# A conv input projection as block pairs of seven products, with modulation sums moved, residual parts added by DMA and fills removed

## The chip, the cores and the metric

The kernel runs on one core of a Trainium2 chip. The metric is the device time of one execution in microseconds. The core has five engines that run beside each other: TensorE (PE, matmuls into PSUM), VectorE (DVE), ScalarE (ACT), GpSimd (POOL) and SyncE (SP, which issues most loads). DMAs run on 16 DMA engines that all issuing queues share.

## The reference

A small diffusion transformer of two layers over 256 latent tokens and 256 context tokens, d = 1024, everything in float32. The kernel works on both streams side by side, as 512 columns (`T2`), the latent half first (`S` = 256 each). What matters here:

```python
def _modulate(t, g, shift, scale):
    return _rms(t, g) * (1 + scale) + shift

def _swiglu(h, w13, w2):
    gte, up = jnp.split(h @ w13, 2, axis=-1)
    return (jax.nn.silu(gte) * up) @ w2

def _short_conv_mixer(h, w_in, k, w_out):
    bgate, cgate, xv = jnp.split(h @ w_in, 3, axis=-1)
    return (bgate * _dwconv3(cgate * xv, k)) @ w_out

for i in range(DEPTH):   # layer 0: short conv; layer 1: attention
    mod  = (jax.nn.silu(c) @ mod_w[i] + mod_b[i])       # 9 chunks of d: shift, scale, gate x 3
    lat = lat + 0.5 * gate0 * _swiglu(_modulate(lat, ...), ffn_w13[i, 0], ffn_w2[i, 0])
    lat = lat + gate1 * mixer(_modulate(lat, ...))
    lat = lat + 0.5 * gate2 * _swiglu(_modulate(lat, ...), ffn_w13[i, 1], ffn_w2[i, 1])
    # the context stream cx goes the same way, up to the attention of layer 1
```

`_dwconv3` is a convolution of width 3 along the tokens, channel by channel.

## The kernel before

**Products.** Every float32 operand is split into a high part `hi` (rounded to the format that PE takes in one pass) and a low part `lo` = x - hi: ACT writes `hi` (L107), DVE writes `lo` (L108). One product is then three matmuls, hi hi, lo hi, hi lo (`mm3`, L136 to L138). Activations lie transposed, channels on partitions, so one matmul takes 128 channels by 512 columns (both streams) or 256 (one).

**Stages.** In order: a first stage written out by hand (`FIRST_STEPS`: modulation by PE, first norm, first three FFN blocks); FFN (0,0); the conv mixer; FFN (0,1); FFN (1,0); attention; FFN (1,1) on the latents alone. An FFN goes in thirds of 8, 7 and 7 hidden blocks: the blocks' gate and up products, then a `project` that multiplies them by that third of `w2`, eight output blocks m, and adds each to the residual `x` in `finish` (two `scalar_tensor_tensor` of 128x256 on DVE, L563, out of PSUM, times the modulation gate). In the last third `finish` also runs a `tail`: squares and sums for the next norm, which normalises one stream while PE still does the last two m of the other.

**Block pairs of seven products.** `Pair` computes a gate block and an up block together. Weights are seen as a 2x2 matrix of blocks (two halves of the 1024 input channels by two output blocks), activations as a 2x2 matrix (two halves of channels by two streams), and the product of these takes seven block products for eight, in the manner of Strassen and Winograd: A11, A12, S1 to S4 and A22 with B11, B21, T1 to T4 and B22. One product is 4 x 3 matmuls of 256 columns. The sums cost work elsewhere: per pair POOL negates a piece and issues two accumulating DMAs (L701, L704, L114), DVE makes the weight sums (L723, L731) and splits them (L108), and combines results in `six`, `seven` and `four` (L760, L765, L771); ACT copies partial results out of PSUM (L748, L754, L758). `Blocks.sums` makes T1 to T4 once per stage. A stage that uses pairs begins with two blocks multiplied plainly, stream by stream, while the norm of the second stream and the T sums come in; in between, the first pair's weights are made.

**The conv input before.** `h` is a `Plain` (hi and lo of each channel block). For each m of 8: three products of 8 channel blocks, `pv`, `pc`, `pb` (24 of `mm3`; for m = 0 stream by stream, otherwise 512 columns), then ACT copies `pv` (L1160), DVE multiplies (L1162), ACT and DVE apply the three taps (L1164, L1167, L1171), DVE multiplies by `pb` (L1176) and the result `z` is split. Then `project` with `conv_w_out`.

**Modulation sums.** 224 of them: DVE reduces a row block of `mod_w` (128x1024, 512 KB loaded per pair of sums) with the conditioning vector (L177). `tick(n)` spreads them: each call adds n to an account and issues a sum for each whole unit; `tick(ev)` stands in `project` for the first m. What is still missing when a gate or norm needs its chunk is issued there and then (`gate_of`, `scale_of`, through `mod_ready`).

**Fills.** `fill(n)` issues n matmuls on a tile of ones into an unused bank (L896): 12 at the start (`WARM`), 2 in each of four `add` of `first_sums`, and the steps F2, F2, F4, F5 of `FIRST_STEPS`.

**Order.** Apart from the first stage and the attention heads, a scheduler with a cost model orders each engine's instructions, and pools hand out buffers in that order: 8 for raw weights (`wr`), 4 each for `wh` and `wl`, 3 each of the 128x512 tags `sg` and `gm`, 6 PSUM banks.

Of the kernel before, what the change touches and what calls it, by code (L numbers as in the profile page):

```python
# [16 lines left out]
P = 128  # L17
D = 1024
# [18 lines left out]


FIRST_STEPS = (
# [9 lines left out]
def hybrid_kernel(ctx: ExitStack, tc: tile.TileContext, a: dict, out: bass.AP):  # L49
# [56 lines left out]
    def split(hi, lo, src):  # L106
        nc.scalar.activation(out=hi, in_=src, func=AF.Copy)  # L107
        return nc.vector.tensor_tensor(out=lo, in0=src, in1=hi.bitcast(F32), op=ALU.subtract)  # L108
# [261 lines left out]
    def pick(h, k, c0, c1):  # L370
        return h.at(k, c0, c1)
# [184 lines left out]

    def finish(m, ps, c0, c1, gate, tail, wide=False):
        g = gate(m)
        for s in range(2):
            for o in [s * S - c0] if not wide else range(0, T2 if s == 0 else 0, S):  # L560
                if not c0 <= s * S < c1:
                    continue
                ins = nc.vector.scalar_tensor_tensor(  # L563
                    out=x[:, m, s * S : s * S + S],
                    in0=ps[:, o : o + S],
                    scalar=g[:, m, s : s + 1],
                    in1=x[:, m, s * S : s * S + S],
                    op0=ALU.mult,
                    op1=ALU.add,
                )  # L570
        if tail:
            tail(m, c0, c1)
        return ins.ins

    def ready():

# [111 lines left out]
    class Pair:  # L688
# [67 lines left out]
        def six(self):  # L756
            self.prod(self.p, "S2", "T2", False)
            nc.scalar.copy(self.sg[:, S:], self.p)  # L758
            self.prod(self.q1, "S4", ("B", 1, 1), False)
            nc.vector.tensor_tensor(out=self.sg, in0=self.q, in1=self.sg, op=ALU.add)  # L760
            nc.scalar.activation(out=self.sg, in_=self.sg, func=AF.Silu)  # L761

        def seven(self):
# [4 lines left out]

        def four(self, g):
            self.prod(self.p, "A22", "T4", False)  # L770
            nc.vector.tensor_tensor(out=self.gm, in0=self.sg, in1=self.u, op=ALU.mult)  # L771
            split(g[0], g[1], self.gm)

    def ffn(l, b, h, tot, gate, tail, gs=(), ev=(0, 0), z=None):
        gs = list(gs)
        i0 = 0
        for t, n in enumerate(THIRDS):
            between = ()
            if tot == T2:
                heads = []  # L780
                if t == 0 and not gs:

                    w = [load_w(a["w13"][l, b, 0])]
                    gs = [new_pair("g") for _ in range(2)]
                    pp = [(psum("pg"), psum("pu")) for _ in range(2)]
                    w13_mm(pp[0], w[0], h, range(KT), 0, S)
                    flush(1)
                    w.append(load_w(a["w13"][l, b, 1]))
                    at = w13_mm(pp[1], w[1], h, range(2), 0, S)
                    with tc.issue_after(at):  # L790
                        flush()
                    with tc.issue_after(every[-1]):
                        w13_mm(pp[1], w[1], h, range(2, KT), 0, S)
                    h.sums(0)
                    w13_mm(pp[0], w[0], h, range(KT), S, T2)
                    w13_post(pp[0], gs[0], 0, T2)
                    heads.append(Pair(a["w13"][l, b, 2], h))
                    h.sums(1)
                    heads[0].sums(0)
                    w13_mm(pp[1], w[1], h, range(KT), S, T2)  # L800
                    w13_post(pp[1], gs[1], 0, T2)
                    heads[0].head()
                    heads[0].sums(1)
                    h.sums(2)
# [336 lines left out]
    zs = []  # L1141
    for m in range(KT):
        wcx = load_w(a["cw_cx"][m])
        if m % 2 == 0:
            wb = load_w(a["cw_b"][m // 2])
        pc, pv, pb = psum("pc"), psum("pv"), psum("pb")
        for c0, c1 in ((0, S), (S, T2)) if m == 0 else ((0, T2),):
            groups = ((pv, wcx, P), (pc, wcx, 0), (pb, wb, (m % 2) * P))
            if m == 0:
                order = [(k, *g) for k in range(KT) for g in groups[:2]]  # L1150
                for k in range(KT):
                    order.insert(min(10 + 3 * k, len(order)), (k, *groups[2]))
            else:
                order = [(k, *g) for g in groups for k in range(KT)]
            for n, (k, ps, w, off) in enumerate(order):
                mm3(ps[:, c0:c1], w(k * 256 + off), pick(h, k, c0, c1), k == 0, k == KT - 1)
                if n == 11:
                    flush()
        xv = tp.tile([P, T2], F32, name=nm("xv"), tag="sg", bufs=3)
        nc.scalar.copy(xv, pv)  # L1160
        u = tp.tile([P, T2], F32, name=nm("u"), tag="gm", bufs=3)
        nc.vector.tensor_tensor(out=u, in0=xv, in1=pc, op=ALU.mult)  # L1162
        d = tp.tile([P, T2], F32, name=nm("d"), tag="gm", bufs=3)
# [7 lines left out]
        nc.vector.scalar_tensor_tensor(  # L1171
            out=d2[:, :, : S - 1], in0=u2[:, :, 1:], scalar=convk[:, 2, m : m + 1],
            in1=d2[:, :, : S - 1], op0=ALU.mult, op1=ALU.add,
        )
        z = tp.tile([P, T2], F32, name=nm("z"), tag="sg", bufs=3)
        nc.vector.tensor_tensor(out=z, in0=d, in1=pb, op=ALU.mult)  # L1176
        zs.append(new_pair("z"))
        split(zs[m][0], zs[m][1], z)
        tick(5)

    def by_pairs(key, box=None):
        box = box or {}
# [6 lines left out]

        return ws  # L1190

    hn = Blocks()
# [282 lines left out]
def _layout(inp):  # L1475
# [30 lines left out]
        axis=2,  # L1506
    )
    ci = f("conv_w_in")[0]
    cx = ci[:, D:].reshape(KT, P, 2, KT, P)
    d["cw_cx"] = cx.transpose(3, 1, 0, 2, 4).reshape(KT, P, 2048)  # L1510
    d["cw_b"] = kp(ci[:, :D], 256)
    d["cw_out"] = kp(f("conv_w_out")[0], 256)
# [41 lines left out]
```

## Time and profile before

| | |
|---|---|
| three runs, median (lowest, highest) | 1552.14 us (1551.94, 1553.91) |
| profiled execution | 1552.53 us |
| its span on the core | 1550.8 us |
| busy: PE, DVE, ACT, POOL | 1542.2, 1281.7, 781.8, 223.0 us |
| matmuls | 10238 |
| conv input, first matmul to first matmul of the output projection | 378.5 to 511.3 us |

Busy time of PE overlaps from matmul to matmul, so its pace is read from the distance between starts and not from durations. A window gives, for a stretch in microseconds from the span's start, its length, each engine's busy time (with the count of instructions), the granted TensorE clock, and the mean busy share of the 16 DMA engines.

### The profile page before, as it was taken

The page shows a single profiled execution, that of the slowest core. Times are in us where ns is not written, and L with a number is a line of the kernel's source. Part 1 is how long each engine was busy: PE and PEld are TensorE (multiplying, and loading weights), DVE is VectorE, ACT ScalarE, POOL GpSimd, SP SyncE. Part 2 cuts the span into 40 slices and gives each one's busy share as a digit, 9 for nine tenths or more (in the row PEclk, how much of TensorE's full clock was granted, in tenths as well). Part 3 has the DMA queues.
Part 4 walks back from the last instruction along what each step waited for, and adds up shares of the span by engine and source line. Part 5 has one row for each costly group of instructions (what it writes and reads, how often), then busy time and mean ns, then how long its engine had stood idle before and what let it go on. Part 6 is the DMA issues. An engine that isn't in the chain of part 4 may idle for free.

```text
span 1550.8 us, 26218 instructions
## 1 busy us (share of the span) xinstructions
PE 1542.2 (99%) x10238; PEld 1414.8 (91%) x10238; DVE 1281.7 (83%) x1998; ACT 781.8 (50%) x1294; POOL 223.0 (14%) x187
## 2 busy tenths in 40 slices
PE   9999999999999999999999999999999999999999
PEld 7898998998888899989999899989999899998888
DVE  4888789799987589968978889968978878888676
ACT  5742553544423366436346476436346456774553
POOL 0012213200000112032042112022042002300000
PEclk9999999999999999999999999999999999999999
DMA  9567467475564425655656635655766753376562
GB/s 372 203 184 190 114 187 195 118 197 170 182 208 167 115 63 136 205 145 134 204 144 163 198 75 137 203 150 128 231 174 175 258 165 115 95 234 221 172 196 75
DMA packets 87677, 263.53 MB, mean 170 GB/s; under 512 B 10368, under 2 KB 12032, under 8 KB 87552
## 3 DMA queue, kind: packets, MB, share of 16 engines
q1 hardware_dynamic: 69408, 230.72, 45.8%
q0 software_dynamic: 16128, 29.37, 11.3%
q10 hardware_dynamic: 2016, 1.76, 0.4%
q8 instruction: 80, 1.31, 0.3%
q14 instruction: 45, 0.37, 0.1%
HBM read 259.45 MB, written 1.05 MB: 168 GB/s over the span
## 4 chain that ended last, share of the span: by engine, by line
PE 97%; DVE 1%; ACT 0%; DMA 0%; issue 0%; POOL 0%; SPq 0%; ACTq 0%; POOLq 0%; DVEq 0%
PE py L137 9%; PE py L136 9%; PE py L138 9%; PE p L138 7%; PE p L137 7%; PE p L136 7%; PE q L138 5%; PE q L136 5%; PE q L137 5%; PE py L144 2%; PE pu L144 2%; PE pg L144 2%; PE py L146 1%; PE pg L146 1%; PE pu L146 1%; PE pv L136 1%
## 5 line engine op out<-in xcount | busy, mean ns | idle before, releaser
L107 ACT ACTIVATE wh<-wr 128x1024 fp32r<-128x1024 f32 (+2 forms) x434 | 388.1, 921 | 335.3 <-PE py L137 129.0
L108 DVE TENSOR_TENSOR wl<-wr,wh 128x1024 fp32r<-128x1024 f32 (+2 forms) x434 | 450.5, 1061 | 84.0 <-ACT wh L107 65.0
L177 DVE CUSTOM_DVE_ANT_0 junk<-wr,scbc,first 128x1024 bf16<-128x1024 f32 x213 | 274.7, 1290 | 8.5 <-DMA wr<-in_modT 6.6
L137 PE MATMUL py<-gl,wh 128*128 128x512 f32 (+1 forms) x570 | 213.4, 374 | 0.0
L136 PE MATMUL py<-gh,wh 128*128 128x512 f32 (+1 forms) x570 | 213.3, 374 | 0.0
L138 PE MATMUL py<-gh,wl 128*128 128x512 f32 (+1 forms) x570 | 212.9, 373 | 0.0
L701 POOL TENSOR_SCALAR wr<-wr 128x512 f32<-128x512 f32 x56 | 102.6, 1832 | 533.2 <-DMA wr<-in_w 258.3
L563 DVE SCALAR_TENSOR_TENSOR x<-py,mod,x 128x256 f32<-128x256 f32 x213 | 94.3, 479 | 66.5 <-PE py L138 55.0
L137 PE MATMUL p<-tl,wh 128*128 128x256 f32 x448 | 126.8, 283 | 0.0
L138 PE MATMUL p<-th,wl 128*128 128x256 f32 x448 | 126.8, 283 | 0.0
L136 PE MATMUL p<-th,wh 128*128 128x256 f32 x448 | 126.7, 283 | 0.0
L138 PEld LDWEIGHTS py<-gh,wl 128*128 128x128 f32 x570 | 107.3, 188 | 19.3
L136 PEld LDWEIGHTS py<-gh,wh 128*128 128x128 f32 x570 | 107.4, 188 | 18.2
L137 PEld LDWEIGHTS py<-gl,wh 128*128 128x128 f32 x570 | 107.4, 188 | 18.1
L114 POOL DMA_DIRECT2D w4l<-in_w x56 | 54.2, 967 | 447.8 <-ACT w4l L113 421.4
L137 PE MATMUL q<-bl,wh 128*128 128x256 f32 x320 | 90.6, 283 | 0.0
L138 PE MATMUL q<-bh,wl 128*128 128x256 f32 x320 | 90.6, 283 | 0.0
L136 PE MATMUL q<-bh,wh 128*128 128x256 f32 x320 | 90.6, 283 | 0.0
L137 PEld LDWEIGHTS p<-tl,wh 128*128 128x128 f32 x448 | 86.0, 192 | 0.4
L136 PEld LDWEIGHTS p<-th,wh 128*128 128x128 f32 x448 | 86.0, 192 | 0.3
L138 PEld LDWEIGHTS p<-th,wl 128*128 128x128 f32 x448 | 86.0, 192 | 0.0
L761 ACT ACTIVATE sg<-sg 128x512 f32<-128x512 f32 x56 | 35.3, 631 | 90.5 <-DVE sg L760 90.5
(316 smaller groups left out, 4070.4 us busy)
## 6 DMA issues: line engine op xcount, KB each, us to landing
wr<-in_w SPq DMA_DIRECT2D x120, 512.0 KB, 4.6
wr<-in_modT SPq DMA_DIRECT2D x117, 512.0 KB, 4.8
wr<-in_w2b SPq DMA_DIRECT2D x64, 448.0 KB, 4.0
wr<-in_w2a SPq DMA_DIRECT2D x32, 512.0 KB, 4.7
wr<-in_w SPq DMA_DIRECT2D x56, 256.0 KB, 3.8
wr<-in_w POOLq DMA_DIRECT2D x56, 256.0 KB, 5.7
w4l<-in_w POOLq DMA_DIRECT2D x56, 256.0 KB, 5.8
pm<-in_mod SPq DMA_DIRECT2D x16, 512.0 KB, 10.0
```

What stands on the lines that cost most here:

```text
L107: nc.scalar.activation(out=hi, in_=src, func=AF.Copy)
L108: return nc.vector.tensor_tensor(out=lo, in0=src, in1=hi.bitcast(F32), op=ALU.subtract)
L114: nc.gpsimd.dma_start(out=lo, in_=src, accum_op=ALU.add)
L136: nc.tensor.matmul(ps, wh, mh, start=first, stop=False, **kw)
L137: nc.tensor.matmul(ps, wh, ml, start=False, stop=False, **kw)
L138: return nc.tensor.matmul(ps, wl, mh, start=False, stop=last, **kw).ins
L144: nc.tensor.matmul(ps, w[0], m[2], start=first and n == 0, stop=False)
L146: nc.tensor.matmul(ps[:, :S], w[1], m[0], start=False, stop=last and n == len(ms) - 1)
L177: nc.vector.tensor_tensor_reduce(out=junk, in0=raw, in1=scbc[:, v, :], scale=0.5 if ch in (2, 8) else 1.0, scalar=modb[:, l, col : col + 1 ...
L563: ins = nc.vector.scalar_tensor_tensor(out=x[:, m, s * S : s * S + S], in0=ps[:, o : o + S], scalar=g[:, m, s : s + 1], in1=x[:, m, s * S ...
L701: nc.gpsimd.tensor_scalar(out=r1[:, :T2], in0=r2[:, :T2], scalar1=-1.0, scalar2=None, op0=ALU.mult)
L761: nc.scalar.activation(out=self.sg, in_=self.sg, func=AF.Silu)
```

## The change

Four parts.

1. *Conv input as pairs.* The 24 output blocks (c, x and b of eight m) become 12 parts: eight `Conv` (c and x of one m) and four `Gates` (b of two m), in the order Conv, Conv, Gates. The first two Conv are taken plainly in the opening (two products of 8 channel blocks each, stream by stream); the other ten parts are pairs of seven products. `taps` applies u = x c and the three taps in place, in the pair's own buffers (`sg` and `gm`), and the results wait in `ds` until the Gates part multiplies them and splits z. The FFN's opening becomes the function `opening`, used by both. `h` becomes a `Blocks`. The conv output projection is entered with the last pair's `seven` and `four` between its first products, and its weights are loaded per m.
2. *Modulation sums.* `tick(5)` per m of the conv (40 in all) becomes `tick(0.5)` per pair (5). The projections' `ev`: first FFN (3, 3) to (4, 3.4), conv output 2.5 to 4, second FFN (2.9, 2.7) to (3.6, 3).
3. *Residual parts.* In `finish`, for 512 columns and without a tail (the first two thirds of three FFNs, 48 outputs): ACT scales PSUM into a buffer of tag `sg` or `gm`, and POOL issues a DMA that adds it to `x`, in place of two DVE instructions.
4. *Fills.* The 2 in each `add` and the first F2 of `FIRST_STEPS` go, its second F2 goes, and F4 becomes F2.

```diff
 FIRST_STEPS = (
-    "L10 L00 R00 R10 F2 X U0 P10 L11 F2 P00 L01 F4 T0 W00 N00 W01 N01 F5 h000 w000 l000 R20 W10 "
+    "L10 L00 R00 R10 X U0 P10 L11 P00 L01 F2 T0 W00 N00 W01 N01 F5 h000 w000 l000 R20 W10 "
...
     def finish(m, ps, c0, c1, gate, tail, wide=False):
         g = gate(m)
+        if c1 - c0 == T2 and not tail:
+            t = tp.tile([P, T2], F32, name=nm("yg"), tag="sg" if m % 2 else "gm", bufs=3)
+            for s in range(2):
+                c = slice(s * S, s * S + S)
+                nc.scalar.activation(
+                    out=t[:, c], in_=ps[:, c], func=AF.Copy, scale=g[:, m, s : s + 1]
+                )
+            nc.gpsimd.dma_start(out=x[:, m, :], in_=t, accum_op=ALU.add)
+            return
...
+    def opening(h, srcs, post):
+
+        w = [load_w(srcs[0])]
+        pp = [(psum("pg"), psum("pu")) for _ in range(2)]
+        w13_mm(pp[0], w[0], h, range(KT), 0, S)
+        flush(1)
+        w.append(load_w(srcs[1]))
+        at = w13_mm(pp[1], w[1], h, range(2), 0, S)
+        with tc.issue_after(at):
+            flush()
+        with tc.issue_after(every[-1]):
+            w13_mm(pp[1], w[1], h, range(2, KT), 0, S)
+        h.sums(0)
+        w13_mm(pp[0], w[0], h, range(KT), S, T2)
+        post(pp[0], 0)
+        head = srcs[2]()
+        h.sums(1)
+        head.sums(0)
+        w13_mm(pp[1], w[1], h, range(KT), S, T2)
+        post(pp[1], 1)
+        head.head()
+        head.sums(1)
+        h.sums(2)
+        return head
...
             for i in range(4):
                 nc.tensor.matmul(
...
-            fill(2)
...
-    hn = Plain()
-    ffn(0, 0, h, T2, gate_of(0, 0), tail_norm(0, 1, hn), gs0, (3, 3))
+    hn = Blocks()
+    ffn(0, 0, h, T2, gate_of(0, 0), tail_norm(0, 1, hn), gs0, (4, 3.4))
...
-    for m in range(KT):
-        wcx = load_w(a["cw_cx"][m])
...
-                mm3(ps[:, c0:c1], w(k * 256 + off), pick(h, k, c0, c1), k == 0, k == KT - 1)
...
-        z = tp.tile([P, T2], F32, name=nm("z"), tag="sg", bufs=3)
-        nc.vector.tensor_tensor(out=z, in0=d, in1=pb, op=ALU.mult)
-        zs.append(new_pair("z"))
-        split(zs[m][0], zs[m][1], z)
-        tick(5)
+    def taps(m, c, x, sg, gm):
+
+        u, d = (sg, gm) if m % 2 else (gm, sg)
+        nc.vector.tensor_tensor(out=u, in0=x, in1=c, op=ALU.mult)
+        ds[m] = d
         nc.scalar.activation(out=d, in_=u, func=AF.Copy, scale=convk[:, 1, m : m + 1])
...
+    class Conv(Pair):
...
+        def post(self, g):
+            taps(self.m, self.u, self.sg, self.sg, self.gm)
+
+    class Gates(Pair):
...
+        def post(self, g):
+            for m, out, b in ((self.m, self.sg, self.sg), (self.m + 1, self.gm, self.u)):
+                nc.vector.tensor_tensor(out=out, in0=ds[m], in1=b, op=ALU.mult)
+                zs.append(new_pair("z"))
+                split(*zs[m], out)
+
+    parts = [lambda m=m: Conv(m, h) for m in range(KT)]
+    for i in range(KT // 2):
+        parts.insert(3 * i + 2, lambda i=i: Gates(i, h))
+    prev = None
+    for n in range(2, len(parts)):
+        if n == 2:
+            pr = opening(h, [a["cw_cx"][0], a["cw_cx"][1], parts[2]], conv_post)
+        else:
+            pr = parts[n]()
+            pr.sums(0)
+            pr.sums(1)
+            pr.head()
+        pr.five()
+        at = prev.seven().ins if prev else None
+        pr.six()
+        if prev:
+            prev.four(None)
+        prev = pr
+        tick(0.5, at)
+    between = (prev.seven, lambda: prev.four(None))
...
     hn = Blocks()
     project(
-        by_pairs("cw_out"), lambda k, c0, c1: (zs[k][0][:, c0:c1], zs[k][1][:, c0:c1]), KT,
-        gate_of(0, 1), tail_norm(0, 2, hn), T2, 2, 2.5,
+        ws_out, lambda k, c0, c1: (zs[k][0][:, c0:c1], zs[k][1][:, c0:c1]), KT,
+        gate_of(0, 1), tail_norm(0, 2, hn), T2, 2, 4, between,
     )
     h = hn
     hn = Blocks()
-    ffn(0, 1, h, T2, gate_of(0, 2), tail_norm(1, 0, hn), (), (2.9, 2.7))
+    ffn(0, 1, h, T2, gate_of(0, 2), tail_norm(1, 0, hn), (), (3.6, 3))
```

The host lays out `cw_cx`, `cw_b` and `cw_out` to match.

More of the change, by code (lines that the diff above doesn't have):

```diff
@@ L760, in six, with act @@
             nc.vector.tensor_tensor(out=self.sg, in0=self.q, in1=self.sg, op=ALU.add)
+            self.act()
+        def act(self):
             nc.scalar.activation(out=self.sg, in_=self.sg, func=AF.Silu)
@@ L781, in ffn @@
                 if t == 0 and not gs:
-                    w = [load_w(a["w13"][l, b, 0])]
                     gs = [new_pair("g") for _ in range(2)]
[L785 to L804, printed above, removed]
+                    heads.append(opening(
+                        h, [a["w13"][l, b, 0], a["w13"][l, b, 1], lambda: Pair(a["w13"][l, b, 2], h)],
+                        lambda pp, i: w13_post(pp, gs[i], 0, T2),
+                    ))
                 prev = None
@@ L1134, in hybrid_kernel @@
         sinT = cload("sinT", [P, S])
-    hn = Plain()
-    ffn(0, 0, h, T2, gate_of(0, 0), tail_norm(0, 1, hn), gs0, (3, 3))
+    hn = Blocks()
+    ffn(0, 0, h, T2, gate_of(0, 0), tail_norm(0, 1, hn), gs0, (4, 3.4))
     h = hn
-    zs = []
-    for m in range(KT):
-        wcx = load_w(a["cw_cx"][m])
[L1144 to L1155, printed above, removed]
-                mm3(ps[:, c0:c1], w(k * 256 + off), pick(h, k, c0, c1), k == 0, k == KT - 1)
[L1157 to L1163, printed above, removed]
+    zs, ds = [], {}
+    def taps(m, c, x, sg, gm):
+        u, d = (sg, gm) if m % 2 else (gm, sg)
+        nc.vector.tensor_tensor(out=u, in0=x, in1=c, op=ALU.mult)
+        ds[m] = d
         nc.scalar.activation(out=d, in_=u, func=AF.Copy, scale=convk[:, 1, m : m + 1])
@@ L1174, in hybrid_kernel, with conv_post, __init__, act @@
         )
-        z = tp.tile([P, T2], F32, name=nm("z"), tag="sg", bufs=3)
-        nc.vector.tensor_tensor(out=z, in0=d, in1=pb, op=ALU.mult)
-        zs.append(new_pair("z"))
-        split(zs[m][0], zs[m][1], z)
-        tick(5)
+    def conv_post(pp, m):
+        xv = tp.tile([P, T2], F32, name=nm("xv"), tag="sg", bufs=3)
+        nc.scalar.copy(xv, pp[0])
+        taps(m, pp[1], xv, xv, tp.tile([P, T2], F32, name=nm("u"), tag="gm", bufs=3))
+    class Conv(Pair):
+        def __init__(self, m, h):
+            super().__init__(a["cw_cx"][m], h)
+            self.m = m
+        def act(self):
+            pass
+        def post(self, g):
+            taps(self.m, self.u, self.sg, self.sg, self.gm)
+    class Gates(Pair):
+        def __init__(self, i, h):
+            super().__init__(a["cw_b"][i], h)
+            self.m = 2 * i
+        def act(self):
+            pass
+        def post(self, g):
+            for m, out, b in ((self.m, self.sg, self.sg), (self.m + 1, self.gm, self.u)):
[22 more added lines that the diff above has]
+    between = (prev.seven, lambda: prev.four(None))
     def by_pairs(key, box=None):
@@ L1190, in by_pairs, with ws_out @@
         return ws
+    def ws_out(m):
+        w = load_w(a["cw_out"][m], 1024)
+        return lambda k: w(k * P)
     hn = Blocks()
     project(
[L1194 to L1195 removed]
+        ws_out, lambda k, c0, c1: (zs[k][0][:, c0:c1], zs[k][1][:, c0:c1]), KT,
+        gate_of(0, 1), tail_norm(0, 2, hn), T2, 2, 4, between,
     )
@@ L1508, in _layout @@
     ci = f("conv_w_in")[0]
[L1509 to L1512, printed above, removed]
+    cx = ci[:, D:].reshape(2, KT // 2, P, 2, KT, P)
+    d["cw_cx"] = cx.transpose(4, 2, 0, 3, 1, 5).reshape(KT, P, 2048)
+    cb = ci[:, :D].reshape(2, KT // 2, P, KT // 2, 2, P)[:, :, :, :, ::-1]
+    d["cw_b"] = cb.transpose(3, 2, 0, 4, 1, 5).reshape(KT // 2, P, 2048)
+    d["cw_out"] = kp(f("conv_w_out")[0], P)
     d["convk"] = f("conv_k")[0].reshape(3, KT, P).transpose(2, 0, 1)
```

4 lines of the change are left out of this document (2 added, 2 removed).

## Prediction, before the changed kernel was run

> **What bounds it now.** I read the page first: busy time and the chain that ended last.
>
> ```profile
> span 1550.8 us, 26218 instructions
> ...
> PE 1542.2 (99%) x10238; PEld 1414.8 (91%) x10238; DVE 1281.7 (83%) x1998; ACT 781.8 (50%) x1294; POOL 223.0 (14%) x187
> ...
> PE 97%; DVE 1%; ACT 0%; DMA 0%; issue 0%; POOL 0%; SPq 0%; ACTq 0%; POOLq 0%; DVEq 0%
> ```
>
> TensorE is the bound, with VectorE not far behind. So I need the price of a matmul as the distance between starts, from PE's timeline (start, duration), in the conv stage and in an FFN pair:
>
> ```profile
> 417.71 0.39 PE L137 MATMUL pv<-hl,wh 128*128 128x512 f32 x1
> ...
> 421.34 0.39 PE L138 MATMUL pc<-hh,wl 128*128 128x512 f32 x1
> ...
> 599.74 0.28 PE L136 MATMUL p<-bh,wh 128*128 128x256 f32 x1
> ...
> 602.86 0.28 PE L138 MATMUL q<-th,wl 128*128 128x256 f32 x1
> ```
>
> The first two rows are 16 starts apart: 0.227 us for 512 columns. The others are 26 apart: 0.120 us for 256, so two halves cost 0.240, 6% more than one whole. Then the stretches, with busy time by engine, granted clock and DMA share (first stage; project of the first FFN's first third; of its last third; conv; conv output; FFN pairs):
>
> ```profile
> 12.00:15.00 3.00, 3.00 (x34) 2.64 (x36) 0.77 (x3) 1.01 (x3) 0.00 (x0) 1.00 1.01 388
> 122.70:158.10 35.40, 35.40 (x158) 29.33 (x157) 28.18 (x44) 10.25 (x14) 9.93 (x8) 1.00 0.70 184
> 344.20:377.10 32.90, 32.90 (x190) 28.93 (x188) 32.49 (x57) 14.06 (x21) 0.00 (x0) 1.00 0.60 200
> 378.50:511.30 132.80, 132.78 (x656) 112.96 (x657) 115.43 (x177) 45.80 (x64) 0.00 (x0) 1.00 0.54 177
> 511.30:556.70 45.40, 45.40 (x249) 39.50 (x248) 23.32 (x40) 17.75 (x30) 6.51 (x6) 1.00 0.40 105
> 590.00:640.00 50.00, 50.00 (x415) 49.91 (x415) 45.52 (x61) 32.26 (x54) 10.38 (x9) 1.00 0.61 165
> ```
>
> PE has no gap inside any of them, not even where VectorE is busy 32.49 of 32.90. What PE does wait for is at stage starts (waits of PE, and the chain at the conv start):
>
> ```profile
> PE pv L136 <- ACT hh L309: 1.4, 1, 1.4
> ...
> PE pg L137 <- DVE bl L108: 0.8, 2, 0.4
> ```
>
> ```profile
> 377.02 1.06 ACT wh L107
> ```
>
> **1. Conv projection: -7.85 us.** Before: m = 0 in halves, 144 matmuls of 256 columns; seven more m with 3 x 8 x 3 each, 504 of 512. That is 504 x 0.227 + 144 x 0.120 = 131.7, and the stretch is 132.8. After: the opening takes two blocks in halves, 2 x 2 x 8 x 3 x 2 = 192 of 256; ten pairs of 7 x 4 x 3 = 84 give 840. 1032 x 0.120 = 123.8. All on PE's path.
>
> The Trainium skill, "TensorE: Matmul & The Clock Gate", section on the back-to-back issue gap, gives N/2.4 + 2.5 ns between matmuls, almost no penalty for halves: 215.8 and 109.2 ns, so that this would save 504 x 0.2158 - 888 x 0.1092 = 11.8 us, an estimate from that page. The rows above disagree with it.
>
> **2. Who feeds the pairs.** VectorE's groups (count | busy, mean ns | idle before):
>
> ```profile
> L177 DVE CUSTOM_DVE_ANT_0 junk<-wr,scbc,first 128x1024 bf16<-128x1024 f32 x213 | 274.7, 1290 | 8.5 <-DMA wr<-in_modT 6.6
> L563 DVE SCALAR_TENSOR_TENSOR x<-py,mod,x 128x256 f32<-128x256 f32 x213 | 94.3, 479 | 66.5 <-PE py L138 55.0 <-PE py L146 10.5
> ...
> L108 DVE TENSOR_TENSOR gl<-gm,gh 128x512 fp32r<-128x512 f32 x66 | 46.6, 705 | 0.7 <-ACT gh L107 0.6
> ...
> L771 DVE TENSOR_TENSOR gm<-sg,p 128x512 f32<-128x512 f32 x56 | 38.4, 685 | 21.1 <-PE p L138 21.1
> ...
> L1171 DVE SCALAR_TENSOR_TENSOR d<-u,convk,d 128x510 f32<-128x510 f32 x8 | 6.0, 748 | 0.1
> ```
>
> An FFN pair takes PE 84 x 0.120 = 10.08 us, in which VectorE is busy 45.52/50 x 10.08 = 9.18. A Conv pair has a product u of L771's shape and two taps (0.685 + 2 x 0.748) in place of L771 and a split (0.685 + 0.705): +0.79. A Gates pair has L771 and the split twice: +1.39. Each has 0.5 modulation sums of 1.290 where the FFN pair has 0.9: -0.52. With two Conv to one Gates that is (2 x 0.79 + 1.39)/3 - 0.52 = +0.47, so 9.65 of 10.08 us, 96%. It fits, with less slack than an FFN pair has: the tap results wait in their buffers for the Gates pair, three buffers to a kind, and the next Conv's first copies need those. Bounds 0 to 0.47 x 10 = 4.7 us; I take 0.7, near the lower one, since PE ran without a gap where VectorE worked 32.49 of 32.90.
>
> **3. The start of the conv.** It becomes an FFN opening. The 1.4 us go: an ACT split of 1.06 stood ahead of the first norm output, waiting for PE's last project matmuls; in the new order that split waits for an earlier weight. Openings have their own wait, 0.8 for two, 0.4 each, and VectorE carries the taps and the norm's block sums on top. Bounds 0.4 to 2.5; 1.5. Net +0.1.
>
> **4. Modulation sums.** The number stays 224. In each of the first FFN's first two projects 5 sums (6.5 us) come in, and 16 residual adds of 0.479 (7.7) go; in the second FFN's, 3.5 (4.5 us) come and the same 7.7 go: nothing late. In the last third of the first, 1.2 sums (1.5 us) come in and nothing goes, but the order now puts the sums ahead of the norm rather than into it. At the conv output 12 sums are ticked instead of 7.5, and the next norm's scale forces what its modulation still lacks: 18 stand on VectorE's queue between the last pair's end and the norm, 23.2 us beside the 23.32 of a stretch of 45.40 in which nearly no sum ran before. Behind them in the queue are the last residual adds and squares, for which the norm that opens the next FFN, and so PE, waits. That is 46.5 in 45.4, 1.1 us too much, and the loads of those sums may come late too. Bounds 0 to 2.6; I take 1.0. Each load moves with its sum on SP's queue.
>
> **5. Residual parts by DMA: 0.** 96 VectorE adds become 96 ACT scalings out of PSUM and 48 accumulating POOL DMAs of 256 KB. The nearest rows are an ACT scaling from PSUM of that shape, and on the page the DMA queues (packets, MB, share of 16 engines' span) and POOL's issue of an accumulating DMA:
>
> ```profile
> L1227 ACT ACTIVATE kn<-pq,qg 128x256 f32<-128x256 f32 x2 | 1.0, 478 | 0.0
> ```
>
> ```profile
> q1 hardware_dynamic: 69408, 230.72, 45.8%
> q0 software_dynamic: 16128, 29.37, 11.3%
> ...
> L114 POOL DMA_DIRECT2D w4l<-in_w x56 | 54.2, 967 | 447.8 <-ACT w4l L113 421.4
> ```
>
> ACT: 16 x 0.478 = 7.6 us per project where it works 10.25 of 35.40: covered, and the six PSUM buffers outlast a late copy. POOL: 8 x 0.97, also covered. What follows on POOL are the next pairs' accumulates; in the queue the last residual DMA stands behind the fourth pair's raw, and its staging buffer is next wanted by the third pair's head, two pairs (20 us) into the phase. DMA: q0's 112 accumulates take 0.113 x 1550.8/112 = 1.56 us of all 16 engines each, so 12.5 per project. If that cover is gone: rival B.
>
> **6. Fills: -0.4.** The chain of the first stage:
>
> ```profile
> 12.63 0.89 PE idle L896 x8
> ...
> 14.42 1.00 PE pr L923 x16
> 15.42 0.64 PE idle L896 x4
> 16.06 1.05 PE pr L923 x16
> ```
>
> Fills lie on the chain, 0.89 + 0.64 here, so up to 1.5 us; but the loads stand at a share of 1.01, and the second pr soon waits for its rows. Bounds 0 to 1.5 gained, apart from the clock (rival C); 0.4.
>
> **Sum.** -7.85 + 0.7 + 0.1 + 1.0 + 0 - 0.4 = -6.45. The profiled execution took 1552.53, 1.73 outside its span: 1550.8 - 6.45 + 1.73 = 1546.1. The median of the three runs, 1552.14, lies 0.39 below the profiled one: **1545.7 us**.
>
> **Rivals.** *A, the conv pairs become VectorE's.* In FFN pairs VectorE idles 10.08 - 9.18 = 0.90 us a pair, waiting for PE and ACT. If that idling is needed, a part takes 9.65 + 0.90 = 10.55, and ten cost 4.7 instead of 0.7: 1549.7. For: L771's 21.1 us idle on PE. Against: 32.49 of 32.90. 0.15.
>
> *B, slower: the residual DMAs starve the projects.* The engines work 0.70 x 35.4 = 24.8 us there; plus 12.5, plus 2.5 modulation loads of 0.5 MB (some 0.458 x 1550.8 us / 230.72 MB, 1.6 us each) is 41.3 in 35.4, 5.9 over. Prefetch can slide into the pairs (share 0.61). If half the excess falls on weights that the project itself waits for, six projects cost 18: 1563. It turns slower above 6.45/6 = 1.1 us a project. 0.09. The Trainium skill's "DMA: Bandwidth & Descriptors", section on SWDGE vs HWDGE, says that each DMA engine round-robins between queues, by which weights would get no precedence.
>
> *C, the clock drops without fills.* PE's waits in the first stage grow to about 1 us; at half clock the 4 us of work there would cost 4: 1549.7. Against: 1.00 granted in every stretch. 0.04.
>
> *D, the page's price per matmul:* -11.8 for -7.85, 1541.8. The rows speak against it: 0.02.
>
> **Numbers.** The forecast has 0.70, its own range 1542.5 to 1548.5; A 0.15, B 0.09, C 0.04, D 0.02. 0.2% is 3.1 us, about what a measurement of this kernel tells from no change. Faster (under 1549.0): 0.70, D's 0.02, 0.06 of A, 0.01 of C and 0.02 of B's mild end, 0.81. Same: 0.07 of A and 0.03 of C, 0.10. Slower: 0.07 of B and 0.02 of A beside a late conv output, 0.09. Range 1541.5 to 1551.5: D below, A and C above, B left out.
>
> **What would show it.** Conv, from its first matmul to the first py, near 125 us; pairs of 10.1 us without PE gaps; a start wait near 0.3; PE at the end of the conv output waiting about 1 us; projects of unchanged length. Wrong: PE gaps inside conv pairs that VectorE ends (A), projects longer than 35.4 us or VectorE waiting for loads (B), PE's clock below 1.00 before 25 us (C).

## The result, and the profile after

The changed kernel takes **1549.35 us** (median of 15 runs, 1547.77 to 1551.60), the kernel before 1552.23 beside it (15 runs, median; 1551.94 to 1553.91): 2.9 us less, ratio 0.998 with a 95% interval of 0.9973 to 0.9988. The forecast was 1545.7, that is 6.45 less. The direction was right, less than half of the gain came, and the runs lie further apart than those of the kernel before. The profiled execution took 1548.97.

The page of the changed kernel: span, busy time, queue 0, the chain by engine, and the residual DMAs (count, size, median us to landing).

```profile
span 1547.2 us, 27333 instructions
...
PE 1533.5 (99%) x10594; PEld 1423.6 (92%) x10594; DVE 1298.2 (84%) x1964; ACT 852.2 (55%) x1468; POOL 301.3 (19%) x265
...
q0 software_dynamic: 25920, 47.20, 18.1%
...
PE 89%; DVE 6%; DMA 2%; ACT 1%; issue 1%; POOL 0%; SPq 0%; DVEq 0%; POOLq 0%; ACTq 0%
...
x<-yg POOLq DMA_DIRECT2D x48, 256.0 KB, 7.6
```

The chain held PE for 97% before and now for 89%: VectorE and DMA have come onto it. PE's longest waits say where (wait in total, times, longest; the first and the fourth group were there before, at 0.9 and 0.8 us):

```profile
PE ss L987 <- DVE sq L984: 1.6, 2, 1.4
PE pg L136 <- ACT bh L391: 1.4, 1, 1.4
PE q L136 <- ACT gm L762: 1.2, 1, 1.2
PE pg L137 <- DVE bl L108: 1.2, 3, 0.4
PE q L138 <- DVE wl L108: 1.0, 1, 1.0
```

L391 is the norm that opens the second FFN, behind the conv output; `gm` L762 the first pair of the first FFN's last third; `wl` L108 the first conv pairs. The conv's start wait of 1.4 us (`pv <- ACT hh`) is gone. The stretches of the prediction again (first stage, two projects, conv up to its first `py`, conv output from its third m, FFN pairs):

```profile
12.00:15.00 3.00, 2.59 (x32) 1.64 (x32) 1.64 (x5) 0.87 (x3) 0.00 (x0) 1.00 0.99 377
121.40:157.00 35.60, 35.60 (x160) 29.49 (x159) 29.89 (x40) 15.53 (x28) 14.10 (x14) 1.00 0.87 229
344.50:377.50 33.00, 33.00 (x190) 29.05 (x189) 27.66 (x49) 16.96 (x27) 8.69 (x6) 1.00 0.67 182
377.54:502.06 124.52, 123.00 (x1019) 122.15 (x1017) 116.28 (x162) 79.30 (x135) 29.90 (x24) 1.00 0.48 123
513.14:552.13 38.99, 37.32 (x215) 32.69 (x213) 37.42 (x67) 15.66 (x24) 3.83 (x3) 1.00 0.62 192
590.00:640.00 50.00, 50.00 (x403) 49.28 (x402) 45.60 (x63) 29.61 (x50) 11.86 (x10) 1.00 0.70 190
```

The conv now takes 124.52 us to its first `py`, and PE is idle for 1.5 of them; at the conv output PE is idle for another 1.7, with VectorE busy 37.42 of 38.99. The DMA share in the first project rose from 0.70 to 0.87.

A ledger of one execution each shows where the difference arises: the start of a stage's first matmul in PE's timeline, for before in us, for the others as the distance from before. `no_r` and `late + pairs` are experiments told below.

| first matmul of | before | changed | residual DMAs alone | changed without them (`no_r`) | late + pairs |
|---|---|---|---|---|---|
| first FFN block | 20.00 | -1.33 | -0.46 | -1.50 | -1.35 |
| third m of the first FFN's third project | 344.21 | +0.29 | -0.41 | -1.44 | -1.35 |
| conv | 378.52 | -0.99 | -0.41 | -2.71 | -2.61 |
| FFN (0,1) | 556.74 | -4.61 | -0.42 | -5.95 | -9.01 |
| third m of that FFN's first project | 650.42 | -4.15 | -0.41 | -5.49 | -7.45 |
| FFN (1,1) | 1361.03 | -4.15 | -0.46 | -4.89 | -7.37 |
| its first project | 1407.53 | -3.56 | -0.72 | -4.68 | -6.71 |

For the changed kernel: the fills give 1.33; 1.6 is lost by the third project; 1.28 comes at the conv start; conv and its output take 174.6 in place of 178.2 us, so 3.6; 0.46 is lost in the next opening and 0.59 at FFN (1,1).

### The profile page after: what moved, and what is told of

Its sections match the earlier page's. It is cut to its first block, busy times and chain, and to the rows that moved or that the text cites. A ratio compares the mean times of both kernels' runs of the same rounds, so it can differ in the third digit from the quotient of the medians.

```text
span 1547.2 us, 27333 instructions
## 1 busy us (share of the span) xinstructions
PE 1533.5 (99%) x10594; PEld 1423.6 (92%) x10594; DVE 1298.2 (84%) x1964; ACT 852.2 (55%) x1468; POOL 301.3 (19%) x265
## 3 DMA queue, kind: packets, MB, share of 16 engines
q1 hardware_dynamic: 69408, 228.10, 45.4%
## 4 chain that ended last, share of the span: by engine, by line
PE 89%; DVE 6%; DMA 2%; ACT 1%; issue 1%; POOL 0%; SPq 0%; DVEq 0%; POOLq 0%; ACTq 0%
PE p L138 8%; PE p L137 8%; PE p L136 8%; PE py L137 8%; PE py L136 8%; PE py L138 8%; PE q L138 6%; PE q L136 6%; PE q L137 6%; PE py L144 2%; PE pu L144 2%; PE pg L144 2%; DVE wl L108 1%; DMA wr<-in_w 1%; PE py L146 1%
## 5 line engine op out<-in xcount | busy, mean ns | idle before, releaser
L108 DVE TENSOR_TENSOR wl<-wr,wh 128x1024 fp32r<-128x1024 f32 (+2 forms) x454 | 468.6, 1056 | 107.0 <-ACT wh L107 87.0
L709 POOL TENSOR_SCALAR wr<-wr 128x512 f32<-128x512 f32 x66 | 125.4, 1900 | 424.0 <-DMA wr<-in_w 162.7
L136 PE MATMUL p<-th,wh 128*128 128x256 f32 x528 | 149.5, 283 | 0.0
L138 PE MATMUL p<-th,wl 128*128 128x256 f32 x528 | 149.4, 283 | 0.0
L137 PE MATMUL p<-tl,wh 128*128 128x256 f32 x528 | 149.4, 283 | 0.0
L138 PE MATMUL q<-bh,wl 128*128 128x256 f32 x400 | 113.2, 283 | 0.0
L137 PE MATMUL q<-bl,wh 128*128 128x256 f32 x400 | 113.2, 283 | 0.0
L136 PE MATMUL q<-bh,wh 128*128 128x256 f32 x400 | 113.2, 283 | 0.0
L136 PEld LDWEIGHTS p<-th,wh 128*128 128x128 f32 x528 | 101.3, 192 | 0.4
L566 POOL DMA_DIRECT2D x<-yg x48 | 44.7, 995 | 215.7 <-ACT yg L563 172.4
```

The source lines that it names most:

```text
L136: nc.tensor.matmul(ps, wh, mh, start=first, stop=False, **kw)
L137: nc.tensor.matmul(ps, wh, ml, start=False, stop=False, **kw)
L138: return nc.tensor.matmul(ps, wl, mh, start=False, stop=last, **kw).ins
L566: nc.gpsimd.dma_start(out=x[:, m, :], in_=t, accum_op=ALU.add)
L709: nc.gpsimd.tensor_scalar(out=r1[:, :T2], in0=r2[:, :T2], scalar1=-1.0, scalar2=None, op0=ALU.mult)
```

## The experiments

All times are medians, each with the kernel before run beside it on the same chip (1552.21 to 1552.32). In some runs the mean granted clock is 0.999 or 0.998 and not 1.000: a stretch of a few microseconds ran at half clock, and one of 3.4 us cost 1.5 us (last section). The text says so where it matters.

### One part at a time

**Residual DMAs alone**, on the kernel before:

```diff
+        if c1 - c0 == T2 and not tail:
+            t = tp.tile(... "yg" ...)          # two ACT copies out of PSUM, scaled
+            nc.gpsimd.dma_start(out=x[:, m, :], in_=t, accum_op=ALU.add)
+            return
```

> The kernel before with one part of the change: the 48 residual parts by accumulating DMA. Theory 1 (their transfers stand in the way of the weight loads of the next third's first pair): 0 to 1.5 us slower than before, some runs hit and some not, so that the runs of this kernel lie 2 us or more apart where those of before lie within 0.4. Theory 2 (the prediction's term of 0): 1552.2 us, runs as close together as before's, and the stall at the first pair of a third does not come.

Measured 1551.83 (11 runs, 1551.64 to 1552.50). Theory 2 held: the six projects keep their place in the ledger, and 48 such DMAs are free where they were put into the old kernel.

**The changed kernel without them** (`no_r`; the lines above taken out):

> The changed kernel with its residual parts added by VectorE again, all else kept. Theory 1: the 1.4 us wait at the first pair of the last third goes, loads land as early as before, and the runs lie within 0.5 us of each other. VectorE has 16 adds of 0.479 us more in each project: 29.86 + 7.7 = 37.5 in 35.57, so up to 2 us can come back per project, in the first two projects of two FFNs: between 1547.5 and 1555 us. Theory 2 (the residual DMAs are free, and VectorE was never near the path): 1549.4 us, runs still 4 us apart.

Measured 1547.84 (7 runs, 1546.53 to 1549.41), 1.5 us faster than the changed kernel by medians; the runs of the two overlap, so the size is rough (the best kernel below loses 2.7 us by the same DMAs, without overlap). The wait at the last third went (1.6 us in the ledger), and 16 more adds per project show in PE's waits only by one of 0.4 us (1143.83). The spread stayed at 2.9 us, so that it isn't the residual DMAs' alone: this half of theory 1 fell.

**Fills alone taken out**, from the kernel before (`fill(2)` in `first_sums`, two `F2` of `FIRST_STEPS`, and its `F4` to `F2`):

> The kernel before with one part of the change: the fills taken out of the first stage. The profile of the changed kernel has the first pg matmul 1.33 us earlier. If that is the fills alone: 1552.2 - 1.3 = 1550.9 us. By the prediction's term: 1551.8. If the earlier start came from elsewhere: 1552.2. Granted clock 1.00 in each case.

Measured 1551.18 (11 runs, 1550.73 to 1551.66): 1.1 us, not 0.4, at a clock of 1.00.

**Residual DMAs and more sums in the projects**, without the conv part:

```diff
-    ffn(0, 0, h, T2, gate_of(0, 0), tail_norm(0, 1, hn), gs0, (3, 3))
+    ffn(0, 0, h, T2, gate_of(0, 0), tail_norm(0, 1, hn), gs0, (4, 3.4))
...
-    ffn(0, 1, h, T2, gate_of(0, 2), tail_norm(1, 0, hn), (), (2.9, 2.7))
+    ffn(0, 1, h, T2, gate_of(0, 2), tail_norm(1, 0, hn), (), (3.6, 3))
```

> The kernel before with two parts of the change: residual parts by accumulating DMA, and more modulation sums in the first two FFNs' projects, 4 and 3.4 at a tick in place of 3, 3.6 and 3 in place of 2.9 and 2.7. The conv stays as it was. The residual DMAs alone moved no project (0.0 us at each of six). Theory 1 (the two together fill the DMA engines at the end of a project, and the next third's first weights land late): the third project of the first FFN starts 1 to 2 us later, 1552.5 to 1553.5 us. Theory 2 (the stall needs the conv part, or is an accident of one run): 1551.8 us as with the residual DMAs alone.

Measured **1556.88** (6 runs, 1555.03 to 1560.22): 5 us slower than with the DMAs alone, more than theory 1 said; three of the runs have a clock below 1.000, and the other three are 3.2 to 4.9 us slower. In its profiled run, the quickest of them, 1.7 us are lost before the third project and 1.1 at the norm behind FFN (0,1). The DMAs alone are free, and the same sums in the same projects bring no such wait where the DMAs are out (`no_r`); together they cost. The sums without the DMAs were not run in the kernel before.

**No modulation sums at all**, in the kernel before and in the changed one:

> The kernel before without its 224 modulation sums and the loads of their rows (their values are set to 0.5): what the sums cost where they were. PE's waits in the trace of before are 1.6 us at the conv start and some 0.15 to 0.6 at four norms, none beside a sum: 1551 to 1552 us if the sums were hidden, less only by what their loads hold up.

> The changed kernel without its 224 modulation sums and the loads of their rows (their values are set to 0.5). Theory S (what was lost of the gain, the stall at the third project's end, at the conv output and at the attention output, comes from where the sums and their loads were moved to): all of it goes, and what is left of the conv's 7.97 us of matmuls, 1.3 of the start wait and 1.1 to 1.3 of the fills shows: 8 to 10 us below the kernel before without its sums, 1542 to 1544. Rival (the conv pairs or the residual DMAs cost it by themselves): 3 to 5 us below it, 1546 to 1548.5.

Measured 1554.09 (11 runs, 1552.41 to 1554.29) and 1545.23 (5 runs, 1545.00 to 1545.62): 8.9 us apart by medians. But eight of the eleven runs of the first kernel have a clock of 0.999, and these are the ones from 1553.96 on; at 1.000 the first takes 1552.41 to 1552.80 and the second 1545.00 to 1545.23, so 7.2 to 7.8 us apart. That is near theory S and far from the rival's 3 to 5, but just short of S's 8, and the second time is 1.2 above its bracket. Taking the sums out of the kernel before gains nothing, so they were hidden there; out of the changed one it gains 4.1, and its two waits for `bh` L391 and `gm` L762 are gone. The wait of 1.0 us for `wl` in the first conv pairs stays:

```profile
PE q L138 <- DVE wl L108: 1.0, 1, 1.0
```

### The conv's opening and its pairs

VectorE around the first conv pairs of the changed kernel (in brackets the idle time before a row):

```profile
392.35 1.22 DVE L420 TENSOR_TENSOR hr<-hr,hr 128x1024 f32<-128x1024 f32 x1 [0.58 <-ACT hr L396]
...
400.46 0.74 DVE L1172 SCALAR_TENSOR_TENSOR xv<-u,convk,xv 128x510 f32<-128x510 f32 x1
...
414.76 1.23 DVE L108 TENSOR_TENSOR wl<-wr,wh 128x1024 fp32r<-128x1024 f32 x1
```

Behind the first of these rows there is no idle time up to the last: block sums, weights and the taps of two conv blocks. PE waits for the last row's `wl`. So the taps were issued later (on `no_r`):

```diff
     def conv_post(pp, m):
...
-        taps(m, pp[1], xv, xv, tp.tile(...))
+        late.append(taps(m, pp[1], xv, xv, tp.tile(...)))   # u now, the rest on call
...
         pr.six()
+        while late:
+            late.pop(0)()
```

> The changed kernel with residual parts on VectorE, and the taps of the conv's first two blocks (four instructions of 0.75 us on VectorE) issued after the first pair's third step and not within the opening. In the trace VectorE has no idle time from 392 to 416 us, and the first pairs wait for it, 0.18 and 1.20 us. Theory A (the opening overloads VectorE, later pairs have room): the 1.4 us go, 1546.5 us. Rival (the conv pairs as a whole are at VectorE's limit): the wait moves to a later pair, 1547.8 us.

Measured 1546.95 (5 runs, 1546.82 to 1548.08): 0.9 of the 1.4 us by medians, within the spread of `no_r`. The profiles are clearer: the two waits of 1.4 us became one of 0.5 at 410.68 and one of 0.27 at 432.65, and later pairs have none. Theory A, not quite in size.

**One sum per conv pair in place of 0.5**, on `no_r`:

> The changed kernel with residual parts on VectorE, and 1 modulation sum per conv pair in place of 0.5. By the prediction's count a pair then has 9.65 + 0.65 = 10.30 us of VectorE in 10.08 of PE: 2.2 us lost in ten pairs, as waits of PE inside them. Five sums fewer are then left for the conv output, 6.5 us, whose waits shrink by 1.5 to 2.5: 1547.5 us in sum. If the pairs have more room than counted: 1545.5 to 1546.3. If they need VectorE's idle time (rival A of the prediction): over 1549.

Measured 1550.74; nine of eleven runs lie between 1547.76 and 1551.43, and two far above. By its profiled run, the quickest, the conv took 0.7 us more than in `no_r` and had one new wait of 0.55 inside a pair: the pairs have some more room than counted. Of these nine it is the only one at a clock of 1.000. The other eight are slower by up to 3.7 us at 0.998 or 0.999, so part of that is half clock; which waits led to it, no trace shows. Rival A is neither shown nor excluded by this kernel.

### The conv output

**Its weights for pairs of m, as before** (`by_pairs("cw_out")` in place of `ws_out`), on the changed kernel:

> The changed kernel with the conv output's weights loaded for pairs of m as before, in place of one by one. Theory 3 (the 1.6 us wait of the next FFN's first matmul comes from a weight split that stands on ACT's queue ahead of the norm's bh and waits for a weight buffer that PE still reads): the wait changes by over 1 us either way. Theory 4 (it comes from the modulation sums that stand ahead of the norm on VectorE): within 0.3 us of the changed kernel.

Measured 1549.11 (11 runs): no clear difference in the median, though PE's 1.59 us before the next FFN's first matmul shrank to 0.15, with three smaller ones behind it. By the starts, conv and its output up to the next FFN's first project are 1.0 us shorter than in the changed kernel, while its profiled run loses 0.9 us more at the first FFN's third project. In the changed kernel the chain at that wait has an ACT weight split ahead of the norm, and the split waits until PE has read a weight buffer for the last time:

```profile
550.46 0.14 PE py L137
550.60 0.02 issue
550.62 1.06 ACT wh L107
551.68 0.80 ACT bh L391 x2
```

**The same on `no_r` with the late taps** ("late + pairs"):

> The changed kernel with residual parts on VectorE, the conv's first taps late (1546.95 us so far), and the conv output's weights loaded for pairs of m as before. With the residual DMAs in, that took the wait of 1.6 us at the next FFN's first matmul to 0.15 and added three of 0.2 to 0.6 behind it: 1546.3 us here if it adds up, 1546.95 if that was the spread.

Measured **1546.08** (5 runs, 1545.81 to 1546.09; ratio 0.9958, 0.9946 to 0.9971). This beats both kernels, and its runs lie close together. It is 0.9 us below the kernel with the late taps alone, and no run of the one reaches the other. So theory 3 held: the split's buffer sets this wait, and loading the weights per m has its part in it. Without any sums the wait goes too; in what way the sums share in it, no run shows.

**Sums earlier**, on `no_r`:

```diff
-                        tick(0.9, at)
+                        tick({(0, 0): 1.3, (0, 1): 1.1}.get((l, b), 0.9), at)
...
-        gate_of(0, 1), tail_norm(0, 2, hn), T2, 2, 4, between,
+        gate_of(0, 1), tail_norm(0, 2, hn), T2, 2, 2.4, between,
```

> The changed kernel with residual parts on VectorE, and the modulation sums put earlier: 1.3 per pair in the first FFN and 1.1 in the second, in place of 0.9, and 2.4 per tick at the conv output in place of 4. Theory 4 (the sums that stand ahead of the norm at the conv output delay it): the waits of 0.8, 1.6 and 0.3 us there shrink by 1.5 to 2.5 us, and the 0.4 at the attention output goes, where four sums fewer are owed: 1545.0 to 1546.0 us. Theory 3 (a weight split that waits for a buffer delays it): 1547.5 us, and the 1.6 us stays. If the FFN pairs have no room for 0.4 sums more (9.18 + 0.52 = 9.70 of 10.08 us), it is slower than 1548.

Measured 1552.34 (11 runs, 1550.57 to 1553.44), 4.5 us slower. The expectation failed, and the chain of this kernel at the end of the conv output tells why:

```profile
538.51 6.68 DMA wr<-in_w
...
545.22 0.64 ACT w4h L112
...
546.50 0.32 ACT sq L260
...
547.32 1.01 PE ss L269 x4
```

VectorE had been idle for 3.5 us by then. The last square, which the norm needs, stands on ACT's queue behind `w4h`, a weight copy for the next FFN, and that weight's load was issued at 538.51, once a `wr` buffer came free, and landed 6.7 us later. PE waited 3.4 us for it, and about 2.5 more went at half clock behind the wait (last section). **With the late taps and 3.3 per tick**:

> The changed kernel with residual parts on VectorE, the conv's first taps late, sums of 1.3 and 1.1 per pair in the first two FFNs, and 3.3 per tick at the conv output, so that none is left for the last moment there (with 2.4 two were, and a weight load for the next FFN, which waited for a buffer that a sum held, came 6.7 us late to ACT, ahead of a square that the norm needs: 3.4 us). Theory W (sums that are late hold weight buffers and so the weights that ACT waits for): the 3.4 us go, and the waits at the conv output are under 1.5 us together: 1545.0 to 1546.5 us. Rival (more sums per pair cost by themselves): 1547.5 or more.

Measured 1551.77 (11 runs, 1550.97 to 1553.29), 4.8 us slower than with the late taps alone. Theory W's cure failed too: PE waits 4.3 us at the same place, behind a load issued at 540.69 that took 7.36 us; and 1.55 and 1.13 us in pairs of the first FFN (105.65 and 271.40), so that more sums per pair cost there too. All runs of these two kernels with earlier sums have a clock of 0.998 or 0.999. The late load is in both chains; that the sums cause its lateness isn't shown by them, only that without any sums the wait doesn't come.

### What the residual DMAs collide with

The best kernel with the DMAs for all m, for m < 4 alone, and for m = 4 to 7 alone:

> The kernel with late first taps and the conv output's weights for pairs of m (1546.08 us with residual parts on VectorE), with the residual parts by accumulating DMA again. If the DMAs cost what they cost beside the moved sums (1549.35 - 1547.84 = 1.5 us): 1547.6 us, and its runs 1 us or more apart again. If they are free and the 1.5 was the conv output's spread: 1546.1.

> The same with residual parts by accumulating DMA for m below 4 alone, and on VectorE for m = 4 to 7. Theory Q (the late DMAs, of m = 4 to 7, wait on GpSimd's queue for ScalarE's copies, and the next third's weight work stands behind them): nothing is lost, 1546.1 us, or less since VectorE is relieved. Theory V (the volume on the DMA engines is what counts): half of the cost, 0.7 us.

> The same with residual parts by accumulating DMA for m = 4 to 7 alone. Theory Q: the whole cost, 1.5 us, 1547.6. Theory V: half, 1546.8.

Measured 1548.79, **1550.09** and 1547.19 (11, 11 and 6 runs): 2.7, 4.0 and 1.1 us lost. Of the 4.0, about 1.5 is the clock: eight of the eleven runs with m < 4 have 0.999 (1549.49 to 1552.44) and the other three 1547.67 to 1548.28, while ten of the eleven with all DMAs have 1.000. What is left is 2.5 us for the early half and 1.1 for the late one, beside 2.7 for the whole. Both theories fell, Q since the early DMAs cost more than the late ones, V since that half costs far more than 0.7. In the second project of the first FFN, the best kernel without DMAs, then with those of m < 4 (VectorE is the third figure behind the length, the DMA share the last but one):

```profile
235.00:245.00 10.00, 10.00 (x46) 8.28 (x45) 9.93 (x18) 3.27 (x4) 0.00 (x0) 1.00 0.64 189
245.00:255.00 10.00, 10.00 (x46) 8.29 (x45) 10.00 (x17) 3.26 (x5) 2.18 (x1) 1.00 0.61 196
```

```profile
235.00:245.00 10.00, 10.00 (x46) 8.27 (x45) 9.89 (x16) 5.35 (x10) 2.60 (x3) 1.00 0.66 186
245.00:255.00 10.00, 10.00 (x46) 8.29 (x45) 6.66 (x12) 1.91 (x4) 0.89 (x2) 1.00 1.02 280
255.00:265.00 10.00, 10.00 (x45) 8.27 (x45) 10.00 (x17) 3.61 (x6) 7.93 (x6) 1.00 0.90 221
```

GpSimd issues three of these DMAs together at 242.37 and the fourth at 250.06. The DMA engines are then full, and VectorE is busy 6.66 us of the 10. VectorE's timeline and the chain of the same kernel say what it waits for:

```profile
253.60 1.09 DVE L108 TENSOR_TENSOR wl<-wr,wh 128x896 fp32r<-128x896 f32 x1 [3.35 <-ACT wh L107]
```

```profile
244.50 8.03 DMA wr<-in_w2b
...
252.61 0.96 ACT wh L107
...
271.81 0.61 DVE wr L731
...
273.87 0.40 PE q L136
```

A project weight takes 8.0 us to land (3.1 in the same window without the DMAs), VectorE waits for its split, and what it lost there it still owes when the next third begins: PE waits 2.6 us at 273.87, and the clock falls behind it. The residual adds of m = 4 to 7 lie in that backlog; with all parts by DMA they are gone, and VectorE is busy 6.96 of 10 us in the third stretch instead of 10.00.

That is not yet the whole cause. In the changed kernel the chain of the same wait runs like this:

```profile
245.56 8.87 DMA wr<-in_w
...
254.61 2.04 POOL wr L709
...
257.05 5.75 DMA wr<-in_w
...
268.12 2.48 DVE wl L108 x2
...
270.62 0.70 DVE wr L731
...
271.39 0.32 ACT wh L107
...
272.36 0.36 ACT gm L762
...
272.76 0.38 PE q L136
```

A weight piece for the pair behind the project lands late (8.87 us; 4.67 for the same piece in `no_r`). But VectorE's weight sum, the row at 270.62, starts only 0.4 us later than in `no_r` (270.21). What differs more is ScalarE's order. In `no_r` it copies `gm` first and splits the weight behind it:

```profile
269.90 0.37 ACT L753 COPY gm<-q 128x256 f32<-128x256 f32 x1 [1.40 <-PE q L138]
270.93 1.06 ACT L107 ACTIVATE wh<-wr 128x1024 fp32r<-128x1024 f32 x1 [0.66 <-DVE wr L722]
```

In the changed kernel the split stands ahead, waits for VectorE's sum, and the copy that PE needs comes at 272.36. In `r_only` the split stands ahead too, and VectorE idles as long between 243 and 265 us (5.95 us; 5.96 in the changed kernel, 0.38 in `no_r`), but its weight sum is done at 268.47 and not at 271.31, and PE doesn't wait. With the moved modulation sums added to `r_only`, and nothing else, it is done at 272.19 and PE waits. So the wait needs a weight sum that is late and a copy that stands behind the split. The order comes from the scheduler, which put it differently when the residual parts changed. No kernel kept the order and changed the DMAs alone, so how much of the 1.5 us is crowded DMA engines and how much this order stays open.

## Why the prediction was wrong

**1. Conv projection, -7.85: right.** In the pairs the distance of 256-column matmuls is 0.120 us (35 starts apart):

```profile
449.74 0.28 PE L138 MATMUL q<-bh,wl 128*128 128x256 f32 x1
...
453.94 0.28 PE L137 MATMUL q<-bl,wh 128*128 128x256 f32 x1
```

Counted matmul by matmul at the two prices, conv and output are 7.97 us shorter (169.42 for 177.39); 4.3 of these were lost in waits. Conv to its first `py` was to be near 125 us and took 124.52, but that is luck in part: 24 of the 1032 matmuls, 2.9 us, stand behind the first `py`, and 2.2 us of waits took their place. With the measured 0.120 rival D falls, and so does the estimate of 11.8 us from the Trainium skill's "TensorE: Matmul & The Clock Gate".

**2 and 3. Pairs and conv start, +0.7 and +0.1: right in sum.** Opening and first pairs wait 0.21, 0.57, 0.18 and 1.20 us, 2.16 for the 2.2 of the two terms together, and the start wait went as told. Where the loss lies was wrong: the later pairs run without a gap, and the largest wait is in the first pairs, behind an opening with the taps in it.

**4. Modulation sums, +1.0: too small, and by another way.** At the conv output PE lost 1.75 us more than before, in the next opening 0.46, and 0.59 at FFN (1,1), 2.8 in sum. The prediction added up VectorE's work, 46.5 in 45.4 us. The chain of the changed kernel has something else: an ACT weight split that waits for PE to leave a weight buffer and stands ahead of the norm in ScalarE's queue. Loading the weights per m, for which the sum had no term, has its part in that: undoing it gave 0.9 to 1.0 us. In the two kernels with more sums in the pairs it was a late weight load, 6.7 and 7.4 us, ahead of a square on the same queue. The 0.59 has its place at the attention output, where four sums more were still owed (213 of 224 done, 217 before); the prediction followed no sum beyond the conv output.

**5. Residual parts by DMA, 0: the step that failed outright.** It holds for the DMAs alone (1551.83). With the moved sums they cost 1.5 us by medians, 1.6 in the ledger. The term weighed ACT, GpSimd and a mean share of the DMA engines, each as if the other parts of the change weren't there, and it followed GpSimd's queue but not ScalarE's. What the traces show in its place: PE waits 1.4 us for ScalarE's copy of its result, behind a weight split that waits for a weight sum of VectorE, and the moved modulation sums make that late: it is done at 268.47 with the DMAs alone, at 272.19 when the moved sums are added to them and nothing else, and at 271.31 in the changed kernel. Rival B had crowded DMA engines, at 3 us in each of six projects; the one loss came in the pair behind one of them, and the projects kept their length. The loads did get slower, 8.87 us for 4.67, but how much of the wait that is stays open. By the Trainium skill's "DMA: Bandwidth & Descriptors", section on SWDGE vs HWDGE, queues take turns on a DMA engine; a load of 8.0 us for 3.1 beside four residual DMAs is in line with that.

**6. Fills, -0.4: too small**, 1.1 by its own run, at a clock of 1.000 in all eleven runs, against rival C. Rival C's sign did come once, in the profile of the changed kernel without sums: a clock of 0.58 from 7 to 11 us, with the first FFN block 0.35 us later than in the changed kernel.

**Sum by the runs**: fills -1.1; conv and sums together -3.3 (`no_r` less the fills) where the terms 1 to 4 had -6.05; the DMAs +1.5 where they had 0: -2.9. So the larger part of what was missed, 2.75 us, lies in the terms 1 to 4, most of it in term 4; the DMAs are 1.5, and the fills gave 0.7 more than forecast, which hides part of it. Rival A, VectorE as the bound of all pairs, isn't what happened.

## What to carry to other kernels

Work that is moved out of a stage takes its loads along, and it fills the slack of the engine that does it in the new place: price that place with all parts of the change in, not each part alone. Follow who stands behind a late load or a late sum in each in-order queue, ScalarE's above all; a sum of busy times doesn't show that. The DMAs were free alone, and beside the moved sums the two cost 3 to 5 us, so measure the pairs too. Where a scheduler orders the instructions, look whether an edit changed the order elsewhere before calling a resource the cause.

## What the hardware showed beside that

A long wait cost twice here. Where PE waited 3.4 us (sums earlier on `no_r`), it went on at half clock (third figure from the end; then DMA share and GB/s):

```profile
547.00:549.00 2.00, 1.68 (x8) 1.68 (x9) 0.43 (x2) 0.26 (x1) 1.68 (x2) 0.50 0.08 5
...
551.00:553.00 2.00, 2.00 (x11) 2.00 (x11) 1.90 (x5) 1.94 (x4) 0.00 (x0) 0.50 0.69 117
553.00:555.00 2.00, 2.00 (x19) 2.00 (x18) 2.00 (x4) 1.93 (x6) 0.00 (x0) 0.97 0.18 19
```

That is some 5.8 us at half clock, from 547.32 on. A matmul of 256 columns starts every 0.213 us there and not every 0.120, so 27 matmuls took about 2.5 us more. After the 2.6 us wait at 273.87 the clock was 0.50 for 3.4 us, 16 matmuls and 1.5 us. The runs of the kernel before beside the experiments fall into two groups, 1551.81 to 1552.69 at a clock of 1.000 and 1553.69 to 1554.39 at 0.999, which one such stretch would explain. After the changed kernel's 1.6 us the clock stayed at 1.00, and so it did after one of 2.2 us (one sum per conv pair, at 548.78). The Trainium skill's "TensorE: Matmul & The Clock Gate", section "What's actually happening", puts the drop at an idle window of about 3.4 us; here a single wait of 2.6 us was enough, and in the first stage, where PE had done little before it, one of 1.9 us (at 7.36, changed kernel without sums).
